# Two homes in SBUF for the split weight tiles, one of them at the far end

## The chip, the cores and the metric

The kernel runs on one core of a Trainium2 chip. The metric is the device time of one execution in microseconds (us). Five engines work side by side and signal each other by semaphores: TensorE (PE in the profile, its weight loads PEld) multiplies, VectorE (DVE) and ScalarE (ACT) work element by element, GpSimd (POOL) takes some of that, and SyncE (SP) issues DMAs. SBUF is the working memory of 128 partitions; a place in it is given here as a byte of a partition, in KiB of 1024 bytes.

## The reference

A trunk of two layers over 512 tokens of width 1024. Each layer is a half-step SwiGLU feed-forward, a mixer and another half-step feed-forward; the mixer is Mamba-2 in the first layer and windowed attention with sinks in the second; a final RMSNorm ends it. All arrays are float32.

```python
def swiglu(x, w_in, w_out):
    gate, up = jnp.split(x @ w_in, 2, axis=-1)
    return (jax.nn.silu(gate) * up) @ w_out
...
for i in range(DEPTH):
    h = h + 0.5 * swiglu(rms_norm(h, ln_ffn1[i]), ffn1_w_in[i], ffn1_w_out[i])
    u = rms_norm(h, ln_mix[i])
    ...
    h = h + m
    h = h + 0.5 * swiglu(rms_norm(h, ln_ffn2[i]), ffn2_w_in[i], ffn2_w_out[i])
return rms_norm(h, final_norm)
```

## The kernel before

Activations stand transposed, features on partitions and the 512 tokens along them. All weights come in the order of their use as 359 tiles of up to 128 x 1024 float32. Each goes through three steps. load_w (line 183) has SP fetch it into one of two wraw tiles. split_w (from line 187) makes a pair of it: whi, a cast to the matmul's float32r on ACT (line 199), and wlo, the rest wraw - whi (line 200), on DVE or, where the caller hands it over, on POOL. next_w hands the pairs out in order and keeps the splitting two pairs ahead and the loading four.

mm3 (lines 312 to 314) then computes a 128 x 128 block of weights against 512 tokens with three matmuls: whi against the moving tile's high part, whi against its low part, wlo against its high part. With 8 blocks to a pair, project() takes 24 matmuls from each. The moving tile is x (8 tiles, one per 128 features) in the feed-forward's first product and in the mixers' projections, g in the feed-forward's second product (22 tiles per feed-forward), and yt or ot in out_proj, which multiplies the mixers' outputs. In z_next, Mamba's gate, the roles change: x is stationary (the operand that is loaded into the array) and whi or wlo moves, 256 columns at a time (lines 631 to 633). Lines 393 and 546 are transposes by a matmul with the identity cst, in which a tile of x's place (line 393) or of m4's (line 546) is the stationary operand.

A new pair can be written when the last matmul on the pair that stood in its place before is done. In the feed-forward pairs come free in the order in which they were made. In Mamba out_proj takes two pairs at once (out_w) and keeps them over other projections, so there pairs come free in another order. The order of all work is written out by hand (MAMBA_ORDER, SWA_ORDER) and by the loops.

SBUF is laid out pool by pool in the order in which the pools are opened. Of the kernel before, in a partition: the eight x tiles (4 KiB each) at 36.6 to 68.6 KiB, the two wraw tiles behind them, four whi tiles at 76.6 to 92.6 KiB and four wlo tiles at 92.6 to 108.6 KiB; then the group t2 (7 tiles of work space) from 110.6 KiB, and the group m4 (22 tiles of 4 KiB: g, yt, ot, and Mamba's and attention's tiles) at 127.3 to 215.3 KiB, with small tiles behind it up to 223.1 KiB. The starts of x, whi and wlo are whole multiples of 64 bytes; those of m4 lie 32 bytes past one.

Of the kernel before, what the change touches and what calls it, by code (L numbers as in the profile page):

```python
# [12 lines left out]
F32R = mybir.dt.float32r  # L13
# [135 lines left out]
def trunk(ctx: ExitStack, tc: tile.TileContext, xT, pos, wflat, params, consts, out):  # L149
# [3 lines left out]
    cpool = ctx.enter_context(tc.tile_pool(name="const", bufs=1))  # L153
    wpool = ctx.enter_context(tc.tile_pool(name="w", bufs=3))
    mpool = ctx.enter_context(tc.tile_pool(name="m", bufs=1))
    psum = ctx.enter_context(tc.tile_pool(name="ps", bufs=1, space=bass.MemoryType.PSUM))
    dram = ctx.enter_context(tc.tile_pool(name="scr", bufs=1, space=bass.MemoryType.DRAM))

# [18 lines left out]
    def load_w():  # L177
        i = state["load"]
        if i >= len(WIDTHS):
            return  # L180
        w, off = WIDTHS[i], state["off"]
        r = wpool.tile([128, 1024], F32, name="wraw", tag="wraw", bufs=2)
        nc.sync.dma_start(r[:, :w], wflat[off:off + 128 * w].rearrange("(p w) -> p w", w=w))
        raws[i] = r
        state["load"], state["off"] = i + 1, off + 128 * w

    def split_w(eng=None):
        i = state["split"]
        if i >= len(WIDTHS):
            return  # L190
        while state["load"] <= i:
            load_w()
        w, r = WIDTHS[i], raws.pop(i)
        hi = wpool.tile([128, 1024], F32R, name="whi", tag="whi", bufs=4)
        lo = wpool.tile([128, 1024], F32R, name="wlo", tag="wlo", bufs=4)
        if i < KT // 2:
            dve.tensor_copy(hi[:, :w], r[:, :w])  # L197
        else:
            act.copy(hi[:, :w], r[:, :w])  # L199
        (eng or dve).tensor_sub(lo[:, :w], r[:, :w], hi[:, :w].bitcast(F32))  # L200
        split[i] = (hi, lo)
        state["split"] = i + 1
# [3 lines left out]
    def next_w(eng=None):  # L206
        i = used[0]
        used[0] = i + 1
        while state["split"] <= min(i + 2, len(WIDTHS) - 1):
            split_w(eng)  # L210
        while state["load"] <= min(i + 4, len(WIDTHS) - 1):
            load_w()
        return split.pop(i)
# [674 lines left out]
```

## Time and profile before

| | |
|---|---|
| runs (us) | 2124.76, 2128.52, 2128.64; median 2128.52 |
| profiled execution: span from first to last instruction | 2120.2 us |
| what lies around the span, median less span | 8.3 us |
| busy: PE / DVE / ACT / POOL | 98% / 53% / 35% / 10% of the span |
| DMA | 197.62 MB, mean 93 GB/s |

The profiled execution's own time is known by its span; the runs are timed apart from it. Busy shares are averages over stages. A matmul's busy time in the profile reaches over into the next matmul, so how fast PE goes is read from the distance between starts.

### The profile page before, as it was taken

How to read it: one execution, taken by the hardware profiler on the slowest of the kernel's cores; microseconds unless marked ns; L12 is line 12 of the kernel's file. 1: busy time of each engine (PE TensorE's matmuls, PEld its weight loads, DVE VectorE, ACT ScalarE, POOL GpSimd, SP SyncE). 2: the span in 40 equal slices, each digit the busy share in tenths (PEclk: the TensorE clock that was granted, in tenths of full speed). 3: DMA queues.
4: the chain of work that ended last, by engine and by line, in shares of the span. 5: the costliest groups of instructions: out<-in, count | busy, mean ns of one | idle time of the engine just before them, and what ended most of it. 6: DMA issues, size and time to landing. Idle time of an engine off the chain costs nothing.

```text
span 2120.2 us, 24892 instructions
## 1 busy us (share of the span) xinstructions
PE 2081.0 (98%) x9967; PEld 1730.6 (82%) x9967; DVE 1122.2 (53%) x1709; ACT 735.9 (35%) x1088; POOL 201.7 (10%) x142
## 2 busy tenths in 40 slices
PE   8999999999999999999999999999999999999998
PEld 6888888888888877888888888888878878888887
DVE  6443333688888888434433545343366775434333
ACT  4332222454444434322322323222236443322222
POOL 2000001233222222000000000000111120000000
PEclk9999999999999999999999999999999999999999
DMA  5232222433333332333323323322221113333221
GB/s 166 93 99 100 92 95 84 111 91 115 87 97 100 91 89 70 100 99 93 97 90 98 96 95 105 100 91 94 95 91 49 60 42 109 99 100 97 91 94 67
DMA packets 58867, 197.62 MB, mean 93 GB/s; under 512 B 6656, under 2 KB 6912, under 8 KB 58752
## 3 DMA queue, kind: packets, MB, share of 16 engines
q1 hardware_dynamic: 58608, 196.03, 29.4%
q8 instruction: 78, 1.28, 0.2%
q14 instruction: 37, 0.30, 0.0%
q10 hardware_dynamic: 144, 0.00, 0.0%
HBM read 193.85 MB, written 2.16 MB: 92 GB/s over the span
## 4 chain that ended last, share of the span: by engine, by line
PE 83%; DVE 12%; ACT 2%; issue 2%; DMA 1%; POOL 1%; SPq 0%; ACTq 0%; DVEq 0%; POOLq 0%
PE mm L312 25%; PE mm L313 25%; PE mm L314 25%; DVE acc L502 2%; DVE wlo L200 2%; PE psy L574 1%; DVE x L249 1%; DVE h L429 1%; DVE y L580 1%; PE psz L631 1%; PE psz L633 1%; PE psz L632 1%; PE pav L772 1%; DVE y L581 1%; PE pss L740 1%
## 5 line engine op out<-in xcount | busy, mean ns | idle before, releaser
L199 ACT CAST whi<-wraw 128x1024 fp32r<-128x1024 f32 (+2 forms) x355 | 364.9, 1029 | 1071.5 <-PE mm L313 696.4
L312 PE MATMUL mm<-x,whi 128*128 128x512 f32 x1760 | 689.6, 392 | 5.7 <-DVE whi L197 5.6
L313 PE MATMUL mm<-x,whi 128*128 128x512 f32 x1760 | 687.1, 390 | 5.9 <-DVE x L249 5.9
L314 PE MATMUL mm<-x,wlo 128*128 128x512 f32 x1760 | 686.3, 390 | 1.0 <-DVE wlo L200 0.9
L200 DVE TENSOR_TENSOR wlo<-wraw,whi 128x1024 fp32r<-128x1024 f32 (+3 forms) x329 | 396.7, 1206 | 293.6 <-ACT whi L199 281.6
L313 PEld LDWEIGHTS mm<-x,whi 128*128 128x128 f32 x1760 | 330.8, 188 | 76.5 <-DVE x L249 9.1
L312 PEld LDWEIGHTS mm<-x,whi 128*128 128x128 f32 x1760 | 330.9, 188 | 75.7 <-ACT ss L257 5.6
L314 PEld LDWEIGHTS mm<-x,wlo 128*128 128x128 f32 x1760 | 330.7, 188 | 71.4 <-DVE wlo L200 1.9
L312 PE MATMUL mm<-g,whi 128*128 128x512 f32 (+1 forms) x726 | 282.9, 390 | 0.0
L314 PE MATMUL mm<-g,wlo 128*128 128x512 f32 (+1 forms) x726 | 282.7, 389 | 0.0
L313 PE MATMUL mm<-g,whi 128*128 128x512 f32 (+1 forms) x726 | 282.7, 389 | 0.0
L261 POOL TENSOR_TENSOR ss<-ss,sq 128x512 f32<-128x512 f32 x48 | 72.7, 1514 | 1487.3 <-ACT sq L260 1486.0
L346 DVE TENSOR_TENSOR t<-mm,t 128x512 f32<-128x512 f32 x88 | 60.9, 691 | 270.1 <-PE mm L314 269.7
L344 DVE TENSOR_TENSOR t<-mm,rbc 128x512 f32<-128x512 f32 x88 | 60.6, 691 | 214.5 <-PE mm L314 213.5
L313 PEld LDWEIGHTS mm<-g,whi 128*128 128x128 f32 x726 | 136.7, 188 | 31.4
L312 PEld LDWEIGHTS mm<-g,whi 128*128 128x128 f32 x726 | 136.7, 188 | 31.3
L314 PEld LDWEIGHTS mm<-g,wlo 128*128 128x128 f32 x726 | 136.7, 188 | 31.3
L200 POOL TENSOR_TENSOR wlo<-wraw,whi 128x1024 fp32r<-128x1024 f32 x30 | 73.7, 2456 | 230.3 <-ACT whi L199 220.9
L502 DVE SCALAR_TENSOR_TENSOR acc<-xp,par,acc 128x512 f32<-128x512 f32 x96 | 84.5, 880 | 2.1 <-ACT acc L500 1.5
L631 PE MATMUL psz<-whi,x 128*128 128x256 f32 x224 | 64.6, 288 | 5.8 <-DVE xp L498 5.7
L429 DVE TENSOR_TENSOR h<-mm,h 128x512 f32<-128x512 f32 x88 | 59.8, 685 | 19.0 <-PE mm L314 18.6
L363 DVE SCALAR_TENSOR_TENSOR t<-mm,rbc 128x512 f32<-128x512 f32 x31 | 21.5, 692 | 79.9 <-PE mm L314 79.9
(211 smaller groups left out, 1949.2 us busy)
## 6 DMA issues: line engine op xcount, KB each, us to landing
wraw<-wflat SPq DMA_DIRECT2D x320, 512.0 KB, 3.5
wraw<-wflat SPq DMA_DIRECT2D x32, 384.0 KB, 2.9
abc<-actr SPq DMA_DIRECT2D x32, 256.0 KB, 5.8
h<-xT SPq DMA_DIRECT2D x8, 256.0 KB, 3.5
out<-out SPq DMA_DIRECT2D x4, 512.0 KB, 2.7
wraw<-wflat SPq DMA_DIRECT2D x4, 256.0 KB, 2.8
wraw<-wflat SPq DMA_DIRECT2D x2, 432.0 KB, 3.0
cst<-consts SPq DMA_DIRECT2D x1, 321.5 KB, 4.4
```

The costliest lines, as they stand in the source:

```text
L199: act.copy(hi[:, :w], r[:, :w])
L200: (eng or dve).tensor_sub(lo[:, :w], r[:, :w], hi[:, :w].bitcast(F32))
L261: pool.tensor_add(ss, ss, sq)
L312: pe.matmul(ps, whi, xt[:, 0, :], start=first, stop=False)
L313: pe.matmul(ps, whi, xt[:, 1, :], start=False, stop=False)
L314: pe.matmul(ps, wlo, xt[:, 0, :], start=False, stop=last)
L344: dve.tensor_mul(t, pg, rbc)
L346: dve.tensor_mul(t, pu, t)
L363: dve.scalar_tensor_tensor(t, ps, 0.5, rbc, op0=ALU.mult, op1=ALU.mult)
L429: dve.tensor_add(h[m], ps, h[m])
L502: dve.scalar_tensor_tensor(acc, xp[:, j:j + S], pcol(P_CW + t * 4 + j), acc, op0=ALU.mult, op1=ALU.add)
L631: pe.matmul(pz, x[k][:, 0, ts], hi[:, sl], start=k == 0, stop=False)
```

## The change

split_w takes its tiles from two pools in turn. Pairs with an even number (counted from 0) stay in pool w, which now holds two whi and two wlo tiles; pairs with an odd number go to the new pool wfar, which is opened last of the SBUF pools and holds two of each.

```diff
     mpool = ctx.enter_context(tc.tile_pool(name="m", bufs=1))
+    wfar = ctx.enter_context(tc.tile_pool(name="wfar", bufs=2))
     psum = ctx.enter_context(tc.tile_pool(name="ps", bufs=1, space=bass.MemoryType.PSUM))
...
         w, r = WIDTHS[i], raws.pop(i)
-        hi = wpool.tile([128, 1024], F32R, name="whi", tag="whi", bufs=4)
-        lo = wpool.tile([128, 1024], F32R, name="wlo", tag="wlo", bufs=4)
+        home = (wpool, wfar)[i % 2]
+        hi = home.tile([128, 1024], F32R, name="whi", tag="whi", bufs=2)
+        lo = home.tile([128, 1024], F32R, name="wlo", tag="wlo", bufs=2)
```

In a partition of the changed kernel the even pairs lie at 76.6 to 92.6 KiB (whi, then wlo) and the odd ones at 207.1 to 223.1 KiB, with starts 32 bytes past a multiple of 64. All that lies behind pool w, the groups t2 and m4 and the small tiles, starts 16 KiB lower: m4 at 111.3 to 199.3 KiB, its offsets within 64 bytes as before.

Every engine has the same instructions in the same order. Some waits change. In 349 of the 359 pairs the pair whose place is taken is the same as before. In ten it is another one: before, a new pair took the place that came free first among four; now it takes the one of its own home. The ten are five couples in Mamba, each where the two pairs that out_proj held come free: pairs 97 and 98, 105 and 106, 113 and 114, 121 and 122, 129 and 130. Pair 97 took the place of pair 92 and now takes that of 93; pair 98 took that of 93 and now takes that of 92; the last matmul on 93's whi comes three matmuls behind that on 92's.

These are ACT's rows around the first couple before; the casts are those of pairs 96, 97 and 98 in this order, acc and bc belong to the convolution of Mamba's C, and the words in brackets are the semaphores waited for (PE_49 is PE's).

```order
L199 CAST whi<-wraw 128x1024 [waits DMAHW0_49,PE_49,Activation_49]
L500 ACTIVATE acc<-xp,par 128x512 [waits DVE_49,Pool_49]
L199 CAST whi<-wraw 128x1024 [waits DMAHW1_49,PE_49]
L504 ACT_TABLE_LOAD
L504 ACTIVATE bc<-acc,par 128x512 [waits DVE_49]
L199 CAST whi<-wraw 128x1024 [waits DMAHW6_49,PE_49]
```

The same place in the changed kernel, whose lines stand two lower in the file:

```order
L201 CAST whi<-wraw 128x1024 [waits DMAHW0_49,PE_49,Activation_49]
L502 ACTIVATE acc<-xp,par 128x512 [waits DVE_49,Pool_49]
L201 CAST whi<-wraw 128x1024 [waits DMAHW1_49,PE_49]
L506 ACT_TABLE_LOAD
L506 ACTIVATE bc<-acc,par 128x512 [waits DVE_49]
L201 CAST whi<-wraw 128x1024 [waits DMAHW6_49]
```

No instruction moved. The last cast has lost its wait for PE, since the cast two rows above it now waits for the later of the two pairs, and with it for both.

POOL makes wlo of pair 98 and of its like. Here are its rows around the couple of pairs 113 and 114 before: the memset readies the convolution's xp, the first wlo is that of pair 112, the second that of pair 114, the third that of pair 115.

```order
L497 MEMSET xp 128x3 [waits DVE_49] x2
L200 TENSOR_TENSOR wlo<-wraw,whi 128x1024 [waits DVE_49,PE_49,DMAHW0_49,Activation_49,Pool_49]
L200 TENSOR_TENSOR wlo<-wraw,whi 128x1024 [waits DMAHW6_49,PE_49,Activation_49]
L497 MEMSET xp 128x3
L200 TENSOR_TENSOR wlo<-wraw,whi 128x1024 [waits DVE_49,PE_49,DMAHW7_49,Activation_49,Pool_49]
```

And in the changed kernel:

```order
L499 MEMSET xp 128x3 [waits DVE_49] x2
L202 TENSOR_TENSOR wlo<-wraw,whi 128x1024 [waits DVE_49,PE_49,DMAHW0_49,Activation_49,Pool_49]
L202 TENSOR_TENSOR wlo<-wraw,whi 128x1024 [waits PE_49,DMAHW6_49,Activation_49,Pool_49]
L499 MEMSET xp 128x3
L202 TENSOR_TENSOR wlo<-wraw,whi 128x1024 [waits DVE_49,DMAHW7_49,PE_49,Activation_49]
```

The order is the same; the second wlo now also waits for POOL itself, since POOL wrote the tile that stood there before.

## Rows read from the trace of the kernel before

**Rows 1.** The page's busy time and chain that ended last, and the cores view.
```profile
PE 2081.0 (98%) x9967; PEld 1730.6 (82%) x9967; DVE 1122.2 (53%) x1709; ACT 735.9 (35%) x1088; POOL 201.7 (10%) x142
...
PE 83%; DVE 12%; ACT 2%; issue 2%; DMA 1%; POOL 1%; SPq 0%; ACTq 0%; DVEq 0%; POOLq 0%
...
core 0: 2120.2 us, clock 0.999
```

**Rows 2.** Groups by line and shape: busy us, mean ns | idle before, releaser.
```profile
L312 PE MATMUL mm<-x,whi 128*128 128x512 f32 x1760 | 689.6, 392 | 5.7 <-DVE whi L197 5.6
...
L312 PE MATMUL mm<-g,whi 128*128 128x512 f32 x682 | 270.4, 396 | 0.0
...
L199 ACT CAST whi<-wraw 128x1024 fp32r<-128x1024 f32 x320 | 335.7, 1051 | 918.0 <-PE mm L313 549.5 <-issue 349.6 <-DMA wraw<-wflat 9.5
```

**Rows 3.** Timeline of PE, x moving, first and last of 178.
```profile
1299.80 0.39 PE L312 MATMUL mm<-x,whi 128*128 128x512 f32 x1
...
1339.91 0.39 PE L312 MATMUL mm<-x,whi 128*128 128x512 f32 x1
```

**Rows 4.** Timeline of PE, g moving, first and last of 169.
```profile
1459.62 0.39 PE L312 MATMUL mm<-g,whi 128*128 128x512 f32 x1
...
1498.98 0.39 PE L312 MATMUL mm<-g,whi 128*128 128x512 f32 x1
```

**Rows 5.** Timeline of PE, 256 columns: 23 of psz, 66 of g.
```profile
558.89 0.28 PE L632 MATMUL psz<-wlo,x 128*128 128x256 f32 x1
...
561.52 0.28 PE L633 MATMUL psz<-whi,x 128*128 128x256 f32 x1
...
2091.74 0.28 PE L312 MATMUL mm<-g,whi 128*128 128x256 f32 x1
...
2099.36 0.28 PE L314 MATMUL mm<-g,wlo 128*128 128x256 f32 x1
```

**Rows 6.** Weight loads of two lines: duration min/median/max ns, first and last start.
```profile
L393 PEld LDWEIGHTS pso<-cst,y x16: 139/140/142, 2108.2 to 2109.9; 128*128 128x128 f32 x16
...
L546 PEld LDWEIGHTS psx<-cst,xc x64: 139/141/142, 429.7 to 789.4; 128*128 128x128 f32 x64
```

**Rows 7.** Writes of g by DVE: duration min/median/max ns.
```profile
L349 DVE TENSOR_TENSOR g<-t,g x88: 682/684/695, 36.4 to 1985.7; 128x512 fp32r<-128x512 f32 x88
```

**Rows 8.** Timeline of all engines at one of the five places.
```profile
544.15 0.40 PE L313 MATMUL mm<-yt,whi 128*128 128x512 f32 x1
...
544.59 1.05 ACT L199 CAST whi<-wraw 128x1024 fp32r<-128x1024 f32 x1 [3.17 <-PE mm L313]
...
544.85 0.40 PE L313 MATMUL mm<-yt,whi 128*128 128x512 f32 x1
...
545.66 1.28 ACT L504 ACT_TABLE_LOAD   x1
...
546.90 1.21 DVE L200 TENSOR_TENSOR wlo<-wraw,whi 128x1024 fp32r<-128x1024 f32 x1
...
547.58 1.03 ACT L199 CAST whi<-wraw 128x1024 fp32r<-128x1024 f32 x1
...
548.69 2.39 POOL L200 TENSOR_TENSOR wlo<-wraw,whi 128x1024 fp32r<-128x1024 f32 x1 [5.38 <-ACT whi L199]
...
549.01 2.88 DVE L580 TENSOR_TENSOR y<-y,xds 128x768 f32<-128x768 f32 x1
...
551.93 1.22 DVE L581 TENSOR_TENSOR y<-y,zs 128x1024 f32<-128x1024 f32 x1
...
558.69 0.36 PE L631 MATMUL psz<-whi,x 128*128 128x256 f32 x1
```

**Rows 9.** Timeline of DVE and POOL 94 us earlier.
```profile
454.84 0.96 DVE L580 TENSOR_TENSOR y<-y,xds 128x768 f32<-128x768 f32 x1
...
456.14 2.40 POOL L200 TENSOR_TENSOR wlo<-wraw,whi 128x1024 fp32r<-128x1024 f32 x1 [8.31 <-ACT whi L199]
...
456.32 3.31 DVE L581 TENSOR_TENSOR y<-y,zs 128x1024 f32<-128x1024 f32 x1
```

## Prediction

> **What bounds the kernel now.** I read the page first. The reader is to see that TensorE (PE) is busy for 2081.0 of 2120.2 us, with VectorE (DVE) at 53% and ScalarE (ACT) at 35%, and that 83% of the chain that ended last lies on PE and 12% on DVE; the granted clock is 0.999 throughout [rows 1]. So nearly every nanosecond that a matmul gains or loses counts, and what ACT, DVE and GpSimd (POOL) lose counts only where PE or that chain waits for it.
>
> The groups by line come next, for the counts. The three lines of mm3 issue 1760 matmuls each with x as the moving operand, 5280 in all, and 682 each with g at 512 columns, 2046 in all [rows 2]. The code adds 3 x (128 + 64) = 576 of out_proj, whose moving operand is yt or ot, so 2622 have a tile of the m4 group. The z products of z_next are 7 groups x 4 chunks x 8 x 3 = 672 matmuls of 256 columns in which the weight tile is the moving operand and x the stationary one.
>
> Third, the timeline, for the step from one matmul's start to the next; the busy time of one (392 ns) overlaps its neighbour's and says nothing of it. With x moving, 177 steps take 1339.91 - 1299.80 = 40.11 us, or 226.6 ns each [rows 3]. With g moving, 168 steps take 39.36 us, or 234.3 ns [rows 4]. Nothing else in these two stretches differs for PE: same shape, same weight homes, no idle time. So the trace shows one place effect already, 7.7 ns per matmul, between x (37 to 69 KiB, starts that are whole multiples of 64 bytes) and m4 (127 to 215 KiB, starts 32 bytes past one). The far home has both properties of m4. That is what makes this change worth a calculation.
>
> **The change part by part.** The span is 2120.2 us; the median of the runs is 2128.5 (2124.8 to 2128.6), so 8.3 us lie around the span, and I work with differences and add them to the median. The program has the same instructions in the same order on every engine, and the same loads. What moves is addresses, and which earlier pair a new one replaces.
>
> *Stationary reads from the far home.* Half of the 5280 + 2622 matmuls of 512 columns, 3951, load weights from the far home. The nearest rows are weight loads of transposes: those of line 393 read x's place (37 to 69 KiB), those of line 546 a tile of m4 (127 to 215 KiB, 32 bytes past a multiple of 64), and they take 140 and 141 ns at the median, with the same lowest value [rows 6]. So a load costs at most 1 ns more there. If each of these nanoseconds reached PE's step, that is 3951 x 1 ns = 4.0 us; if a load hides under the matmul before it, 0. The other bound is the moving operand's price: 7.7 ns for each far load, but only where the moving operand is x, since those with m4 tiles may be paying it already: 2640 x 7.7 = 20.3 us. Below, the sum is bounded by the case that the 7.7 ns belong to the distance between the two operands: 1311 matmuls with m4 tiles get them back, 10.1 us. I take 0: the row that reads a stationary operand from both places is nearer than rows on the moving one.
>
> *Weights as the moving operand.* Half of the 672 z products, 336, now stream from the far home. At 256 columns z steps at 2.63 us / 22 = 119.5 ns from the near home, and the last stage, with g moving, at 7.62 / 65 = 117.2 [rows 5]. By these rows m4's kind of place is 2.3 ns cheaper at 256 columns, or 0.8 us in all; by half of the 7.7 ns it is 1.3 us dearer. I take 0 and keep -0.8 and +1.3.
>
> *The m4 group 16 KiB lower.* Four more of its 22 tiles come to start below 128 KiB; the offsets in 64 bytes stay. If distance from x's place were what costs, 4/22 of 2046 matmuls would gain up to 7.7 ns, 2.9 us. DVE's writes of g, which go through all the tiles of m4, lie between 682 and 695 ns [rows 7], so I see no place effect on the writing side and take 0 for the casts and subtractions that write far tiles too. Even 13 ns on each of about 340 would be 4.4 us on engines that are half idle.
>
> *The five places in Mamba.* Here the order of release changes (the rows are in the section on the change). Pair 97 took the home of pair 92; it now takes that of pair 93, whose last matmul on whi starts at 544.85 instead of 544.15 [rows 8]: three steps, 0.70 us. ACT's cast sits on that wait (it starts at 544.59, just as pair 92 is done), so it goes to 545.29. Behind it on ACT are the table load, bc's activation and the cast of pair 98, back to back: all move by 0.70. Pair 97's own wlo on DVE starts at 546.90; its cast would end at 546.34, so it is hidden with 0.56 us to spare. The first matmul on pair 97 is at 558.69, far behind. The raw load that waits for pair 98's wlo moves by the same 0.70; of the casts' 918.0 us of idle time loads end 9.5 [rows 2], so I take it as hidden.
>
> What is not hidden is POOL: pair 98's wlo starts at 548.69 and would start at 549.39. Rows 8 and 9 show what that means. Line 580 on DVE takes 0.96 us with POOL quiet, and line 581 took 3.31 where POOL's wlo had started 0.18 us ahead of it: 456.14 + 2.40 = 458.54, and 1.09 more is its end at 459.63 [rows 9]. In the other order line 580, which started 0.32 us behind POOL, took 2.88: POOL's end at 551.08 plus 0.81 is its end at 551.89 [rows 8]. So DVE stands still while POOL holds. If the same holds the other way, line 580 now starts first, at 549.01, ends at 549.97, POOL's wlo runs from there to 552.36, and line 581 ends at 552.36 + 1.09 = 553.45 instead of 551.93 + 1.22 = 553.15: 0.30 us late. This is on the chain that ended last in Mamba. Five times is **+1.5 us**. If the two only share, it is 0; if all of the 0.70 came through, 3.5.
>
> The Trainium skill says why such an order matters: its page "SBUF — State Buffer", section "Who interferes with whom", states that a DVE instruction with two SBUF inputs contends with a GpSimd instruction that reads SBUF, and that issue order decides which of them blocks. By that rule the sum is the +1.5; by shared ports without order it would be 0. The two DVE rows agree with the rule in one direction, and none of them shows POOL waiting for DVE.
>
> **Sum:** 0 + 0 + 0 + 1.5 = 1.5 us, and 2128.5 + 1.5 = **2130**, 0.07% over the median and inside what a measurement of this kernel can tell from no change (0.2%, 4.3 us).
>
> **The rivals.**
> *Slower: place taxes the stationary operand as it taxes the moving one.* Place: every matmul with x moving and a far pair, from the second pair on. Price up to 7.7 ns x 2640 = 20.3 us, so 2128.5 + 20.3 + 1.5 = 2150; with a third of it (the weight is a quarter of the moving operand's bytes), about 2137. It decides from 1.1 ns per far matmul (2.8 us on top of 1.5). For it: the far home has the same offset in 64 bytes as m4, and PE has no slack in these stretches. Against it: rows 6. Those are loads for transposes with a step of their own, so it can't be dismissed. Chance 0.22.
>
> *Faster: the 7.7 ns are a matter of both operands lying far apart.* Then far pairs under m4 tiles run at x's step and the x stages stay: 10.1 us less, 2128.5 - 10.1 + 1.5 = 2120. For it: only m4 tiles are slow, and all weights were near x. Against it: the transposes of line 393 and 546 have their other operand, the constants, at one place and load alike [rows 6]; and a step that depends on distance should cost x something when its weights go away, which would eat the gain (2640 x 7.7 is twice 10.1). Chance 0.15.
>
> *The change does nothing but rename addresses:* the five places are hidden as well, 2128.5. It can't be told from my forecast by time, only by the trace; it stands inside the forecast's chance.
>
> **How the numbers follow.** My forecast with that last case has 0.63, the slower rival 0.22, the faster one 0.15; so slower by over 0.2% has 0.22, within 0.2% 0.63 and faster 0.15. The forecast's own range is 2124 to 2133 (the runs' own spread below, +3.5 and the +1.3 of z above). To hold 8 in 10 it must reach into both rivals: down to 2119, which takes the full faster rival, and up to 2142, which takes the slower one to about two thirds of its price.
>
> **What would show it.** Right: steps of 226.6 and 234.3 ns in the same two stretches, under near and far pairs alike; five casts 0.7 us later against their surroundings; line 580 near 1 us and line 581 near 3.5 at those places. Wrong: steps that alternate every 24 matmuls with x moving (one project per pair), which would be the slower rival; every second weight tile of 8 matmul triples at 226.6 under g, the faster one; casts or subtractions that alternate in duration. The prediction fails most easily on the step of x: one nanosecond there over 2640 matmuls is 2.6 us.

## The result and the profile after

The changed kernel takes 2139.05 us (median of four runs, 2138.44 to 2140.76), the kernel before 2127.44 (median of four, 2124.76 to 2128.64) beside it. The ratio is 1.006 with a 95% interval of 1.0046 to 1.0074, which is 11.6 us, between 9.8 and 15.7. So the change made the kernel slower by about 0.6%: inside the range of the prediction, but not its likeliest case.

First the page of the changed kernel (busy time by engine, chain that ended last, groups by line: busy us, mean ns | idle before, releaser) and its cores view. Lines of mm3 and of split_w stand two lower in the file than before.

```profile
PE 2102.0 (98%) x9967; PEld 1735.0 (81%) x9967; DVE 1122.2 (52%) x1709; ACT 736.0 (34%) x1088; POOL 204.1 (10%) x142
...
PE 86%; DVE 10%; issue 1%; ACT 1%; DMA 1%; POOL 0%; SPq 0%; ACTq 0%; DVEq 0%; POOLq 0%
...
L314 PE MATMUL mm<-x,whi 128*128 128x512 f32 x1760 | 696.3, 396 | 5.8 <-DVE whi L199 5.7
...
core 0: 2139.0 us, clock 0.995
```

Beside [rows 1, 2] the reader is to see what did not change: the counts, DVE's and ACT's busy time, the idle time ahead of mm3. What grew is PE's own busy time, by 21 us (a part of it by the clock, see below), and with it PE's share of the chain, from 83% to 86%; its idle time, span less busy, went from 39.2 to 37.0 us. So PE doesn't wait longer; its matmuls take longer. Which ones, the timeline of PE shows in a feed-forward with x moving, at the first matmul of three pairs in a row, 24 matmuls apart:

```profile
1308.27 0.39 PE L314 MATMUL mm<-x,whi 128*128 128x512 f32 x1
...
1313.86 0.39 PE L314 MATMUL mm<-x,whi 128*128 128x512 f32 x1
...
1319.31 0.39 PE L314 MATMUL mm<-x,whi 128*128 128x512 f32 x1
```

The pair from the far home takes 5.59 us, or 232.9 ns a matmul; the one from the near home 5.45 us, or 227.1. Before, every pair stepped at 226.6 [rows 3]. This alternation was named in the prediction as the mark of the slower rival. With g moving, the steps are 234.2 ns under near pairs and 233.1 under far ones, where [rows 4] gave 234.3 for all.

What it adds up to is seen best in the x stage of the feed-forward between Mamba and the sliding window, where the granted clock is 1.00 throughout in both traces. This is PE's timeline in the changed kernel at the stage's first matmul and at the first one with g:

```profile
1208.05 0.39 PE L314 MATMUL mm<-x,whi 128*128 128x512 f32 x1
...
1451.79 0.39 PE L314 MATMUL mm<-g,whi 128*128 128x512 f32 x1
```

These are 243.74 us. The same two matmuls of before lie 240.44 us apart:

```profile
1197.40 0.40 PE L312 MATMUL mm<-x,whi 128*128 128x512 f32 x1
...
1437.84 0.40 PE L312 MATMUL mm<-g,whi 128*128 128x512 f32 x1
```

The stage has 3 x 352 = 1056 matmuls with x, 528 of them under far pairs: 3.30 / 528 = 6.25 ns each.

The five places in Mamba changed as forecast. Here the timeline of ACT, DVE and POOL in the changed kernel, at the place of [rows 8]:

```profile
548.86 1.05 ACT L201 CAST whi<-wraw 128x1024 fp32r<-128x1024 f32 x1 [3.83 <-PE mm L315]
...
552.63 0.96 DVE L582 TENSOR_TENSOR y<-y,xds 128x768 f32<-128x768 f32 x1
553.01 2.83 POOL L202 TENSOR_TENSOR wlo<-wraw,whi 128x1024 fp32r<-128x1024 f32 x1 [6.09 <-ACT whi L201]
553.62 3.30 DVE L583 TENSOR_TENSOR y<-y,zs 128x1024 f32<-128x1024 f32 x1
```

Line 582 (580 before) is the quick one now, 0.96 us where it was 2.88, and line 583 (581) the slow one, 3.30 where it was 1.22. From the first one's start to the second one's end there are 4.29 us, before 4.14: 0.15 us late each time, where I had 0.30.

The two profiled executions differ by 18.8 us of span, more than the medians. Part of this is TensorE's clock. Windows of the changed kernel (length, busy time of each engine with its instructions, granted clock, DMA):

```profile
788.50:795.30 6.80, 5.87 (x34) 4.63 (x33) 6.80 (x11) 2.78 (x4) 0.00 (x0) 1.00 0.22 77
795.30:802.00 6.70, 3.62 (x14) 2.74 (x13) 4.45 (x6) 0.25 (x1) 6.31 (x2) 0.85 0.00 0
802.00:806.00 4.00, 4.00 (x14) 3.44 (x13) 0.85 (x2) 0.37 (x1) 0.17 (x1) 0.50 0.00 0
```

And the stretch of before that has the same wait of PE as the middle row, and the stretch behind it:

```profile
791.30:798.00 6.70, 3.63 (x21) 2.91 (x20) 4.62 (x7) 0.37 (x1) 6.11 (x2) 1.00 0.00 0
798.00:805.00 7.00, 7.00 (x45) 6.25 (x45) 4.68 (x8) 2.00 (x2) 0.00 (x0) 1.00 0.16 34
```

In both kernels PE waits for 3.1 of these 6.7 us. In the changed kernel's execution the granted clock then fell to 0.50, the lower level of 1.2 GHz, and in that of before it stayed at 2.4. The lag between the same instructions of the two traces grows by 3.0 us there, and by 2.35 at another such place near 1601 to 1610 us. This varies between executions of the kernel before too (19 of them, beside the first experiments, took 2122.04 to 2129.07 us, at mean clocks of 0.999 down to 0.995), so it is no part of the change. Without the two, 18.8 - 5.35 = 13.5 us remain.

### The profile page after: what moved, and what is told of

Read it like the earlier page. It is cut to its first block, busy times and chain, and to the rows that moved or that the text cites. A ratio compares the mean times of both kernels' runs of the same rounds, so it can differ in the third digit from the quotient of the medians.

```text
span 2139.0 us, 24892 instructions
## 1 busy us (share of the span) xinstructions
PE 2102.0 (98%) x9967; PEld 1735.0 (81%) x9967; DVE 1122.2 (52%) x1709; ACT 736.0 (34%) x1088; POOL 204.1 (10%) x142
## 4 chain that ended last, share of the span: by engine, by line
PE 86%; DVE 10%; issue 1%; ACT 1%; DMA 1%; POOL 0%; SPq 0%; ACTq 0%; DVEq 0%; POOLq 0%
PE mm L314 26%; PE mm L315 26%; PE mm L316 26%; DVE acc L504 2%; DVE wlo L202 1%; PE psy L576 1%; DVE x L251 1%; DVE y L583 1%; PE psz L633 1%; PE pss L742 1%; PE psz L634 1%; PE psz L635 1%; DVE h L431 1%; PE pav L774 1%; DVE rn L275 1%
## 5 line engine op out<-in xcount | busy, mean ns | idle before, releaser
L316 PE MATMUL mm<-x,wlo 128*128 128x512 f32 x1760 | 693.3, 394 | 0.7 <-DVE wlo L202 0.6
L634 PE MATMUL psz<-wlo,x 128*128 128x256 f32 x224 | 63.2, 282 | 0.0
```

Of the source, the lines that this page charges most:

```text
L316: pe.matmul(ps, wlo, xt[:, 0, :], start=False, stop=last)
L634: pe.matmul(pz, x[k][:, 0, ts], lo[:, sl], start=False, stop=False)
```

## The experiments

All addresses below are those of the built programs, in bytes within a partition. Where a step is given without rows, it is the mean over all pairs of that kind in a trace, from the start of a group of three matmuls of mm3 to the start of what follows, without the first nine matmuls of a pair, in the kernel's matmuls of 512 columns; groups of over 250 ns a matmul, in which PE waited, are left out.

**The far home, 32 bytes further.** A small tile ahead of it gets eight unused elements, so that the odd pairs start on whole multiples of 64 bytes, as x and the near pairs do. All else is the changed kernel.

```diff
-            ea = sm([128, 32], name="ea", bufs=1)
+            ea = sm([128, 40], name="ea", bufs=1)[:, 0:32]
```

> The changed kernel with its far home moved on by 32 bytes, so that its tiles start at whole multiples of 64 bytes; nothing else moves. Theory of the offset: what costs is that a far tile starts 32 bytes past a multiple of 64. Then matmuls with x moving step at 226.6 to 227 ns under far pairs too, and the time comes back to that of before within 2 us (2126 to 2130), the five places in Mamba being all that is left. Rival, theory of the place: what costs is that the far home lies at 207 KiB and above, away from x. Then far pairs keep their step of about 233 ns and the time stays near 2139.

It took 2127.12 us, a ratio to the kernel before of 1.0003 (0.9994 to 1.0013). Its timeline of PE at the starts of three pairs in a row, far and near by turns, has the old step under both kinds:

```profile
1301.53 0.39 PE L314 MATMUL mm<-x,whi 128*128 128x512 f32 x1
...
1306.96 0.39 PE L314 MATMUL mm<-x,whi 128*128 128x512 f32 x1
...
1312.40 0.39 PE L314 MATMUL mm<-x,whi 128*128 128x512 f32 x1
```

5.43 and 5.44 us, 226.5 ns a matmul. So 32 bytes undo the loss while the weights stay some 130 KiB from where they were. The far end and the five places together cost 2.8 us at the most (the interval's upper end).

**The near home, every second pair 32 bytes off.** The kernel before, all weights at home, with tiles 16 elements wider.

```diff
-        hi = wpool.tile([128, 1024], F32R, name="whi", tag="whi", bufs=4)
-        lo = wpool.tile([128, 1024], F32R, name="wlo", tag="wlo", bufs=4)
+        o = 8 * (i % 2)
+        hi = wpool.tile([128, 1040], F32R, name="whi", tag="whi", bufs=4)[:, o:o + 1024]
+        lo = wpool.tile([128, 1040], F32R, name="wlo", tag="wlo", bufs=4)[:, o:o + 1024]
```

> The kernel before, all weights in the near home, but every odd pair's tiles start 32 bytes past a multiple of 64 (tiles of 1040 elements, of which odd pairs use 8 to 1031). The order of release is that of before. Theory of the offset: odd pairs step at about 233 ns with x moving, even pairs at 227, and the time is that of the changed kernel, 2137 to 2141. Theory of the place: every step stays at 227 and the time at 2127.

It took 2140.44 us, a ratio of 1.0065 (1.0048 to 1.0082): the loss without the change. Its steps under x were not of two kinds, though: since a tile is now 4160 bytes long, its start moves by 64 modulo 256 from one place to the next, and there are pairs at 227.0, 229.3, 232.4, 232.9, 233.2 and 234.0 ns, among them some that start on a multiple of 64 and are slow. That was the first sign that "32 past a multiple of 64" is not the rule.

**The m4 tiles, 32 bytes further.** The kernel before, with g, yt and ot on multiples of 64, the other half of the same idea.

```diff
-        rbc = sm([128, S], name="rbc", bufs=1)
+        rbc = sm([128, S + 8], name="rbc", bufs=1)[:, 0:S]
```

(The same at the second place where rbc is made, here and in the next but one.)

> The kernel before with the m4 group (g, yt, ot) moved on by 32 bytes, so that its tiles start at whole multiples of 64 bytes (64 past a multiple of 128); weights and x stay. Theory of the offset: the moving operand's 234.3 ns under g fall to 226.6 to 227, over 2622 matmuls 20 us less, 2107 to 2110. If a multiple of 128 is what counts, no change, 2127. Theory of the place (distance or upper half of SBUF): no change, 2127.

It took 2125.12 us, a ratio of 0.9995 (0.9985 to 1.0005). The timeline of PE, 24 matmuls with g moving:

```profile
1462.35 0.39 PE L312 MATMUL mm<-g,whi 128*128 128x512 f32 x1
...
1467.95 0.39 PE L312 MATMUL mm<-g,whi 128*128 128x512 f32 x1
```

5.60 us, 233.3 ns: hardly less than the 234.3 of [rows 4]. The theory that a tile's own start within 64 bytes sets the step has fallen.

**Sixteen distances in one kernel.** The kernel before, with tiles as in the second experiment and the pair's offset chosen by its number.

```diff
+        o = (0, 0, 8, 8, 4, 4, 12, 12)[i % 8]
```

> The kernel before, all weights near, with the tiles of a pair starting 0, 64, 32, 96, 16, 80, 48 or 112 bytes past a multiple of 128, in turn over eight pairs in the order of use. One look, for the step with x moving by offset. Theory of the offset in 64 bytes: 0 and 64 step at 227, 32 and 96 at about 233, and 16, 48, 80, 112 at 233 or more. If any offset that isn't a multiple of 64 costs alike, all six are at 233; if it goes by the number of 32-byte pieces that a read touches, 16 and 48 differ from 32. Theory of the place: all at 227.

One execution, 2143.06 us. Sorted by each operand's own start, the steps make no sense; sorted by the distance from the moving tile's start to the weight tile's, modulo 256 bytes, x and g fall on nearly the same values but for the distances of 16 and 144, though x starts at 128 and g at 32 modulo 256. This is the table in ns, filled up from the other traces; whi and wlo have the same distance in each:

```
distance mod 256   0      16     32     48     64     80     96     112
under x            226.8  233.1  233.4  233.3  233.1  232.0  234.0  233.1
under g            226.7  230.6  233.1  233.0  233.3  232.1  234.3  233.2

distance mod 256   128    144    160    176    192    208    224    240
under x            232.5  233.2  233.2  230.0  229.2  231.7  232.9  227.0
under g            232.3  230.8  233.2  229.7  229.3  231.9  233.1  228.0
```

The seventh experiment, with other pairs at 16, has 233.1 there under g too; why 16 and 144 differ here is open. Before, x's pairs were at 0 and all pairs of g, yt and ot at 96. In the changed kernel the far pairs are at 224 from x and at 64 from g.

**The m4 tiles, 96 bytes further.** If this is right, g, yt and ot must become quick by the 96 bytes that 32 bytes did not bring. This is the kernel before with one number other than in the third experiment.

```diff
-        rbc = sm([128, S], name="rbc", bufs=1)
+        rbc = sm([128, S + 24], name="rbc", bufs=1)[:, 0:S]
```

> The kernel before with the m4 group moved on by 96 bytes; weights and x stay. The distance from moving to weight tile, taken modulo 256 bytes, is then 0 for g, yt and ot as it has been for x all along (before: 96 for the m4 tiles, 0 for x; with m4 moved on by 32 bytes: 64). Theory of the distance: PE's step depends on that remainder alone and is shortest, 226.8 ns, at 0. Then g, yt and ot step at 226.8 to 227 instead of 234.3, over 2622 matmuls 19 to 20 us less: 2107 to 2109. Rival, a property of the m4 tiles or of the stages that use them (their place in the upper half, 66 matmuls into one bank): step of 233 to 234, time 2125 to 2128.

It took 2109.4 us (2105.62 to 2110.27), a ratio of 0.9919 (0.9903 to 0.9936), 17.2 us less than the 2126.61 beside it, and it beats both kernels. Its page and its timeline of PE:

```profile
PE 2064.1 (98%) x9967; PEld 1731.0 (82%) x9967; DVE 1121.6 (53%) x1709; ACT 735.8 (35%) x1088; POOL 201.6 (10%) x142
```

```profile
1450.06 0.39 PE L312 MATMUL mm<-g,whi 128*128 128x512 f32 x1
...
1455.50 0.39 PE L312 MATMUL mm<-g,whi 128*128 128x512 f32 x1
```

5.44 us, 226.7 ns: g steps as x does. A g stage takes 119.68 us, before 123.70.

**Everything behind the first small tiles, 32 bytes further.** The changed kernel with x, near pairs, m4 and far pairs all moved alike. The far pairs now start on multiples of 64, the near ones and x do not, and all distances stay.

```diff
-    warm = cpool.tile([128, 1], F32, name="warm")
+    warm = cpool.tile([128, 9], F32, name="warm")[:, 0:1]
```

> The changed kernel with x and all that lies behind it moved on by 32 bytes, far home included. Every distance between tiles stays; the far tiles now start at whole multiples of 64 bytes, and x and the near tiles 32 bytes past one. Theory of the distance: nothing changes, near pairs step at 227 and far pairs at 233 with x moving, time 2137 to 2141. Rival, theory of the 64-byte start: the far pairs are now the quick ones at 227 and the near ones the slow ones, and with x itself off a multiple perhaps all are slow (2139 to 2156).

It took 2140.24 us, a ratio of 1.0061 (1.0046 to 1.0076), the changed kernel's. The timeline of PE, first a far pair, then a near one:

```profile
1310.26 0.39 PE L314 MATMUL mm<-x,whi 128*128 128x512 f32 x1
...
1315.85 0.39 PE L314 MATMUL mm<-x,whi 128*128 128x512 f32 x1
...
1321.30 0.39 PE L314 MATMUL mm<-x,whi 128*128 128x512 f32 x1
```

5.59 and 5.45 us, as in the changed kernel. What counts is the distance, not where either tile starts.

**Distances by 4 bytes.** As the fourth, with other offsets.

```diff
+        o = ((0, 1, 2, 3), (12, 13, 14, 15), (0, 5, 10, 15), (0, 5, 10, 15))[i % 4][i // 4 % 4]
```

> The kernel before, all weights near, with starts that vary from pair to pair so that the distance from moving to weight tile modulo 256 takes 0, 4, 8, 12 and 240, 244, 248, 252 bytes, and some between 64 and 188. One look, for the step by distance. Theory of the distance: 226.8 at 0, a smooth rise to about 233 within 16 bytes above 0, and little rise just below (240 gave 227 to 228 before). If only 0 itself is quick, 252 and 4 are at 230 or more. If some remainder is quicker than 0, a step under 226 shows.

One execution, 2146.26 us. Under x: 227.1 ns at 0, but 232.4 at 4, 230.6 at 8, 232.9 at 12; 230.9 at 116, 227.0 at 120, 231.5 at 124; 227.0 at 240 and 233.0 to 233.2 at 244 to 252. There is no smooth rise away from 0, which I had expected. Quick are 0, 120 and 240 alone among the distances that occurred under x, and none is quicker than 0.

**Only the wlo tiles off.** The kernel before, with 32 bytes between whi and wlo, so that of the three matmuls of mm3 only the last has an operand off its distance of 0.

```diff
+        if i == 0:
+            pad = wpool.tile([128, 8], F32, name="pad", tag="pad", bufs=1)
+            pool.memset(pad, 0.0)
         lo = wpool.tile([128, 1024], F32R, name="wlo", tag="wlo", bufs=4)
```

> The kernel before, with 32 bytes between the whi and the wlo tiles: under x, whi lies at a distance of 0 modulo 256 bytes and wlo at 32; under g, whi at 64 and wlo at 96. A group of three matmuls of mm3 is x with whi, x with whi again, x with wlo. If the slow step belongs to the matmul's own two operands, the step from the wlo matmul's start to the next start is about 233 ns and the two others are 226.7. If it belongs to the weight load that runs while the matmul before it still streams, the step from the second whi matmul's start to the wlo matmul's start is about 233 and the two others are 226.7. If two of the three are slow, both streams meet it. By either of the first two, a third of the steps of x is slow, and the one execution takes some 2127 + 7 = 2134 us (1408 of them in the feed-forwards by 6.3 ns is 8.9, and 2046 steps of g give back about 1.5).

One execution, 2147.27 us, where I had 2134. Both theories missed: it is not a third of the steps that is slow. The timeline of PE, twelve matmuls with x moving:

```profile
1300.12 0.40 PE L315 MATMUL mm<-x,whi 128*128 128x512 f32 x1
...
1302.92 0.40 PE L315 MATMUL mm<-x,whi 128*128 128x512 f32 x1
```

2.80 us, 233.3 ns on average, as if all three were off. By position the means are 232.5 and 239.1 ns after the first and second start with whi and 228.3 after that with wlo. With g moving, whi at 64 and wlo at 96, the three average 231.1, less than either distance alone gave (233.3 and 234.3). So one tile that is off slows the matmuls on the other tile too, and the table above holds only where whi and wlo have the same distance.

**The change, with every distance at 0.** The far pairs stay at the far end; it and the m4 tiles are moved to a distance of 0 from all they meet.

```diff
-        rbc = sm([128, S], name="rbc", bufs=1)
+        rbc = sm([128, S + 24], name="rbc", bufs=1)[:, 0:S]
...
-            ea = sm([128, 32], name="ea", bufs=1)
+            ea = sm([128, 80], name="ea", bufs=1)[:, 0:32]
```

> The changed kernel with the odd pairs still at the far end, but 32 bytes further (and 96 for the m4 tiles), so that every weight tile, x, g, yt and ot lie at a distance of 0 modulo 256 bytes. If the distance is all that the change cost, the time is that of the kernel before with m4 moved by 96 bytes, 2109.4 us, within 3 us, a ratio of 0.990 to 0.994 to the kernel before, and x and g both step at 226.7 to 227.2 ns under near and far pairs. If the far end or the five places cost something of their own once the slow steps no longer cover it, it is above that by this amount, 2113 us or more.

It took 2111.04 us (2109.35 to 2113.83), a ratio of 0.9929 (0.9912 to 0.9945). Near and far pairs step alike, 226.75 ns under x and 226.67 under g. Its timeline of PE, over 48 matmuls, as many as a far and a near pair have:

```profile
1289.65 0.39 PE L314 MATMUL mm<-x,whi 128*128 128x512 f32 x1
...
1300.53 0.39 PE L314 MATMUL mm<-x,whi 128*128 128x512 f32 x1
```

10.88 us, 226.7 ns a matmul. The interval overlaps that of the fifth experiment; the 1.6 us between the medians can't be told from nothing. So the place at the far end costs nothing that these runs can tell even where no slow step covers it. The far pairs lie 256 bytes past a multiple of 512 from x here (whi at 212352, x at 37504) and the near ones at a multiple of 512, so the remainder by 256 is what counts and not that by 512.

## Why the prediction went as it did

**Where it failed.** The step is "Stationary reads from the far home", of which I wrote "I take 0: the row that reads a stationary operand from both places is nearer than rows on the moving one". The runs showed 6.25 ns for each far load under x, near the upper bound of 7.7. (The means of far and near pairs in the changed kernel, 232.9 and 227.2, differ by less, 5.7, since the last step of a near pair is slow as well; see below.) [rows 6] misled me for two reasons. They give how long a load takes, and mm3's loads take no longer now; this group of the changed kernel, near and far pairs together (duration min, median, max), has the same median as before, and apart the medians are 188 and 187 ns:

```profile
L314 PEld LDWEIGHTS mm<-x,whi x1760: 186/188/334, 5.7 to 2001.8; 128*128 128x128 f32 x196
```

What grew is the step of the matmuls, on which a load's own row says nothing. And the transposes have other operands at other distances, so they were no measure of a load beside x.

**Beside which matmul.** The changed trace shows where a far load is paid for. Here are matmuls and loads where a near pair gives way to a far one, and where that far one gives way to the next near one:

```profile
1308.03 0.40 PE L316 MATMUL mm<-x,wlo 128*128 128x512 f32 x1
1308.04 0.19 PEld L314 LDWEIGHTS mm<-x,whi 128*128 128x128 f32 x1
1308.27 0.39 PE L314 MATMUL mm<-x,whi 128*128 128x512 f32 x1
...
1313.63 0.39 PE L316 MATMUL mm<-x,wlo 128*128 128x512 f32 x1
1313.64 0.19 PEld L314 LDWEIGHTS mm<-x,whi 128*128 128x128 f32 x1
1313.86 0.39 PE L314 MATMUL mm<-x,whi 128*128 128x512 f32 x1
```

Each pair's first load runs beside the last matmul of the pair before it. Over all such places with x moving and no wait, the step from a near pair's last matmul to a far pair's first is 235.0 ns (86 places), and that from a far pair's last to a near pair's first is 227.1 (93); in the first experiment, with all at a distance of 0, both are 226.8. So at these borders the slow step is not that of the matmul that uses the far weights but that of the matmul beside which they are loaded.

**The rival that came true, with the wrong reason.** The slower rival had the right matmuls, 2640 under x, and nearly the right price for one. That the time lies inside the range is owed to this rival's share in the range; the forecast's own 1.5 us, with loads at nothing, did not come true. The rival's time, 2150, did not either: outside the feed-forwards its matmuls brought next to nothing (see the sum), and it called the price a tax on a place. The first experiment left the place and took the tax away, the second brought the tax to the old place, and the sixth moved every start and changed nothing. What I read in [rows 3, 4] as a place effect of the m4 tiles, 7.7 ns, was their distance of 96 from the weights: 96 bytes of shift removed it. The faster rival, "both operands lying far apart", had the right kind of quantity and took it as kibibytes; far pairs under g got 1.1 of 7.7 ns back, since their distance went from 96 to 64.

**The sum, term by term.** The four feed-forwards hold 4 x 528 = 2112 of the far matmuls under x: 2112 x 6.25 = 13.2 us. Mamba's x has 384 more, but the lag between the two traces grows by only 1.1 us there up to the clock's fall, all that happens in Mamba included: less than half of 384 x 6.25 = 2.4. Most of the 1.1 are the five places, 0.15 us each, 0.75, half of the forecast; the first experiment has them without slow steps, and its line 582 starts 0.05 us later than line 580 of before at the first of them and 0.76 later at the last. That DVE, which is busiest in that stage, hides the far matmuls is argued, not shown. Streaming the weights costs less from the far pairs: z's step (means without waits) is 118.0 ns under far pairs and 119.5 under near ones, 336 x 1.5 = 0.5 us, between the 0 that I took and the bound of -0.8; it too is within the 1.1. It is no gift of the place, since in the first experiment far pairs take 119.6. The attention has the last 144 far matmuls, and the lag grows by 2.2 us there, 0.1 less than the clock alone made. g gives back 0.4 us in each of its four stages, 1.5 in all. The lot is 13.2 + 1.1 - 0.1 - 1.5 = 12.7 us, beside 11.6 measured (9.8 to 15.7) and 13.5 between the two traces.

**The five places.** Order, casts and the two DVE lines came as forecast. The price was half, because POOL was not held back whole: its wlo started 0.38 us into line 582 and took 2.83 us in place of 2.39, ending at 555.84, and line 583 ended 1.08 us behind it (1.09 in [rows 9]). The Trainium skill's page "SBUF — State Buffer", section "Who interferes with whom", has the order of issue decide which of the two blocks. The changed trace agrees, in the direction that was missing before: line 582 takes 0.96 us beside a POOL instruction that started behind it and took 0.44 us more. These 0.44 us are less than the 0.58 that were left of line 582.

**Casts, subtractions, g's writes.** 0 was right: ACT is busy for 736.0 us against 735.9, DVE for 1122.2 in both.

**Around the span.** The "8.3 us around the span" were none: 2140.76 us of one run stand beside a span of 2139.0, so 1.8 lie around it. The profiled execution of before was a quick one. Since I worked with differences, the forecast didn't depend on it.

**What stays open.** Why 256 bytes, why 120 and 240 are quick as well, and how far the effect reaches: if a slow load slowed only the matmul beside it, the eighth experiment would have one slow step in three, the second, but the first took 232.5 ns too.

## What to carry to other kernels

Where TensorE is the bound, read the step from one matmul's start to the next, stage by stage, before looking for waits: two stages of the same shape with 226.7 and 234.3 ns were 17 us of this kernel, and a pad of 96 bytes took them away. When a pool is moved or a tile ahead of it grows, compare the starts of moving and stationary tiles modulo 256 bytes before and after, for matmuls of 512 columns; here a shift that was no multiple of 256 cost more than everything that the edit was about. A price for one operand read from the duration of its own instruction is no price for the pair; measure it as a step, with the partner that it will have.

## What the runs showed of the hardware

- With 512 columns of fp32r, the step of a matmul is 226.7 ns where the moving tile and both weight tiles start at the same byte modulo 256, at each of the three values tried under such pairs (128, 160 and 32), and 229 to 235 at the other distances, but for 120 and 240 (227.0 under x, 228.0 under g at 240) and 212 (236.5).
- At 256 columns 0 is not the quick distance: the last stage's matmuls with g step at 118.0 ns at a distance of 96 (the kernel before), at 115.2 at 64 (the third experiment) and at 119.8 at 0 (the fifth).
- Where near and far pairs meet, the slow step is that of the matmul beside which the far weights are loaded, 235.0 ns, and not that of the matmul that uses them, 227.1.
- The effect is not additive: one of three weight loads off its distance made all three steps 233.3 ns on average, and loads at 64 and 96 in turn made 231.1 where either alone made 233.3 and 234.3.
- Weight loads of 188 ns (median) under a step of 227 or of 233 look the same in their own rows.
- After the same stretch, in which PE waited for 3.1 of 6.7 us, the granted clock fell to 0.50 in one execution and stayed at 1.00 in another.
